# Weights' low halves on VectorE in two pieces, projection products in unbroken halves: a change to the recurrence stage of a transformer block kernel

## The chip, the cores and the metric

One core of one Trainium2 chip. The metric is device time in microseconds (us) of one execution, here the median of several runs. The engines go by the names of the profile: PE (TensorE matmul), PEld (its weight loads), DVE (VectorE), ACT (ScalarE), POOL (GpSimd), SP (SyncE, which issues all DMAs here). "q" behind an engine's name means its queue.

## The reference, cut to what matters

Two transformer blocks on 512 tokens of width 1024, all in float32. The first block is: feed-forward (SwiGLU, inner width 2816), a mixer, feed-forward again. The second is a two-layer hybrid. The change is in the first block's mixer, which projects the normalised input by one wide matrix and feeds the columns to two branches: an RWKV-7 recurrence over time, with 16 heads of 64, and a dilated attention.

```
h = rms_norm(x, mix_norm)
p_rwkv, p_q, p_k, p_v, p_gate = split(h @ w_in)
y_a = rwkv7_time_mix(p_rwkv, ...)
    state = state * w_t + (state @ a_t) b_t + v_t k_t      # 512 steps, per head
    out_t = state @ r_t
y_b = dilated_attention(p_q, p_k, p_v, ...)
merged = g_a * (y_a @ w_proj_rwkv) + g_b * (y_b @ w_proj_attn)
x = x + merged @ w_out
```

## The kernel before, in words

**Products in three parts.** Every large product is made with float32 operands split in a high half (`whi`, `HH`), rounded to the type that PE takes in one pass, and the rest (`wlo`, `HL`). `mm3` (L613) issues three matmuls for one 128x128 block of weights: high by high, high by low, low by high. A block of weights comes as a tile of 128x1024, that is 8 blocks: `wload` (L569) loads it with one DMA on SP into `wraw` (2 buffers), and `wsplit` (L577) makes `whi` by a copy on ACT and `wlo = wraw - whi` by one subtraction of 128x1024 (3 buffers each). The subtraction runs on POOL unless `on` is set; the recurrence stage does not set it. `wnext` (L597) hands out the tile that is due, splits one further tile ahead and loads two ahead (`wfill`, L587).

**The recurrence stage** (`rwkv`, L1175) runs five tasks side by side:

- `rw_stream` (L1233): 24 projection tiles r, k, v, three for each of 8 pairs of heads; `rw_fill` (L1247): 18 tiles of q, k, v for the attention, with a chain of small steps behind each (`qkv_chain`), and 16 tiles of gates. All 58 go through `rw_tile` (L1210): it takes one of two PSUM buffers (`prj`), gets the weights, and issues 8 times `mm3`, 24 matmuls of 512 columns.
- `rw_prep` (L1261): decays, normalised keys and the matrices of 64-step chunks, 8 chunks a pair (`pA` on PE, masked into `AA` on DVE).
- `rw_solve` (L1389), once for each pair: inverts triangular 32x32 blocks. It loads `AS` by 4 DMAs, sets its diagonal (memset on DVE), then 31 times a product `pr` and a sum `Tt` on DVE, each reading the one before; writes `Tt` out by DMA (`scrT`), reads it back transposed (`TB`), makes two groups of 32 small matmuls (`pZ`, a copy on ACT, `pW`, a copy on ACT). `AS` has one buffer, and the copy behind `pZ` lies in it: the next pair's `AS` is loaded only when `pW` is done.
- `rw_chunks` (L1435): the recurrence, 8 chunks for each pair, needs the solve of its pair. A chunk is a chain: `po` on PE, a copy `pp` on ACT, `pu` on PE, a copy into `SV` on ACT, `pS` and a second `po` on PE, and the new state `SV = se + pS` on DVE, with `se` made on POOL.

**What sets the order.** `drive` (L437) plans with estimated durations: each task is a generator that yields the engine it needs next, and the task whose start plus its allowance is least takes the next step. The chunks have allowance 0, the solve 300 ns, the prep 600, `rw_stream` 2000 and `rw_fill` 5000 (`RW_PRIO`, L18). `rw_tile` yields after every `mm3` but the last, so a projection tile is eight steps of 3 matmuls. The framework's scheduler then sets the order of each engine's queue at compile time: of the instructions that its own estimate has ready, the one with the lowest priority number goes first. The number counts up as the program is traced (`cur_priority`); `RW_LATE` (L19) adds 500 to what the two projection tasks issue. Each queue then runs in that fixed order.

Of the kernel before, what the change touches and what calls it, by code (L numbers as in the profile page):

```python
# [7 lines left out]
F32 = mybir.dt.float32  # L8
# [8 lines left out]

RW_PRIO = {"stream": 2000, "fill": 5000}  # L18
RW_LATE = {"rw_stream": 500, "rw_fill": 500, "qkv_chain": -1000}  # L19
FF1_LATE = {"norm": -500, "stats": -300, "mod_steps": 500}  # L20
FF2_PRIO = 300
X_LATE = {"proj_steps": 1000, "taps": 1000, "out_steps": 300}
# [414 lines left out]
def drive(k, tasks):  # L437

    clk, plan, flags = k.clk, k.plan, k.flags
    live = {}
    n = 0

    def hint(x, y):
        x[3] = None
        if isinstance(y, tuple):
            x[3], y = y[:2], y[2]
        x[2] = clk.last
        if y.startswith("+"):  # L450
            y, x[2] = y[1:], 0.0
        x[5] = y.startswith("w")
        x[4] = y.lstrip("w")

    k.born = list(tasks)
    while live or k.born:
        for prio, y, g in k.born:
            live[n] = x = [prio, g, 0.0, None, "PE", False]
            hint(x, y)
            n += 1  # L460
        k.born = []
        if plan.recording:
            best = None
            for i, x in live.items():
                if x[5] and k.held:
                    continue
                r = x[2]
                if x[3] is not None:
                    w = flags.get(*x[3])
                    if w is None:  # L470
                        continue
                    r = max(r, w)
                s = clk.soon(x[4], r) + x[0]
                if best is None or s < best[0]:
                    best = (s, i)
            assert best is not None, ("tasks wait for one another", [(x[1].gi_code.co_name, x[3:]) for x in live.values()])
            i = best[1]
            plan.steps.append(i)
        else:
            i = plan.steps[plan.si]  # L480
            plan.si += 1
        x = live[i]
        assert x[3] is None or flags.get(*x[3]) is not None, "order of tasks"
        clk.last = 0.0
        late = k.late.get(x[1].__name__, 0)
        k.tc._tc.cur_priority += late
        try:
            y = next(x[1])
        except StopIteration:
            del live[i]  # L490
            continue
        finally:
            k.tc._tc.cur_priority -= late
        hint(x, y)
# [32 lines left out]
class K:  # L527
# [49 lines left out]
    def wsplit(self, raw, a, b, on):  # L577
        nc = self.nc
        n = a * b
        hi = self.wp.tile([P, 1024], F32R, tag="whi", name="whi", bufs=3)  # L580
        lo = self.wp.tile([P, 1024], F32R, tag="wlo", name="wlo", bufs=3)
        nc.scalar.copy(hi[:, :n], raw[:, :n])
        (nc.vector if on else nc.gpsimd).tensor_sub(lo[:, :n], raw[:, :n], hi[:, :n].bitcast(F32))
        v = lambda t: t[:, :n].rearrange("p (a b) -> p a b", a=a)
        return v(hi), v(lo)

# [588 lines left out]
    def rwkv(self, H, ya, tw, lad, gd):  # L1175
        nc, tc = self.nc, self.tc
        with ExitStack() as ctx:
# [21 lines left out]
            self.nb["rwmm"], self.nb["qch"] = 2, 1  # L1199
            self.late = RW_LATE  # L1200
            drive(self, [
# [8 lines left out]
    def rw_tile(self, H, w, fin=None, chain=None):  # L1210
        k = self.take("rwmm")
        yield self.need("rwmm", k, "+wPE")
        p = self.rps["mm"].tile([P, T], F32, tag="mm", name="prj")
        w = self.wnext(*w)
        self.held = True
        for x in range(8):
            self.mm3(p, (w[0][:, x], w[1][:, x]), H[x], x == 0, x == 7)
            if x < 7:
                yield "+PE"
        self.held = False  # L1220
        if chain is not None:
            self.spawn(100, "ACT", self.qkv_chain(*chain, p, k))
            return

        def task():
            fin(p)
            self.free("rwmm", k)
            return
            yield

        self.spawn(0, "ACT", task())
# [1191 lines left out]
def body(tc, A, out, plan):  # L2423
    with ExitStack() as ctx:
# [9 lines left out]
        with ExitStack() as lor:  # L2434
            k.lora_setup(lor)
            k.late = FF1_LATE
            with ExitStack() as c2:
# [51 lines left out]
```

## Time and profile before

| | us |
|---|---|
| median of 3 runs | 2654.28 (2636.02 to 2663.36) |
| the profiled execution | 2646.39 |
| its span, first to last instruction | 2644.2 |
| mean granted TensorE clock, share of full speed | 0.927 |

The profiled execution is 2.2 us longer than its span (start and end around the instructions) and lies 7.9 us under the median. The recurrence stage is the stretch from about 442 us, the first projection product, to about 1260 us, the last; the recurrence itself ends at about 1120 us, and what is left of the gate tiles then runs among the attention. All instructions carry the same line (L317, a helper), so groups are told apart by the tiles they write and read: `wlo<-wraw,whi` is the low half of a weight tile.

### The profile page before, as it was taken

What the parts mean: (1) busy time and instruction counts of PE and PEld (TensorE: products, weight loads), DVE (VectorE), ACT (ScalarE), POOL (GpSimd) and SP (SyncE); (2) the same over time, 40 slices, a digit from 0 to 9 for tenths busy, and PEclk for the clock granted to TensorE, in tenths of its full rate; (3) what the DMA queues carried; (4) which work ended last, traced back from release to release, by engine and by line L of the source; (5) the groups of instructions that cost most, each with busy time, mean ns of one, the idle gap of its engine ahead of it and who ended that gap; (6) DMA issues with size and microseconds to landing.
All of it is one profiled execution on the core that took longest, in us unless ns stands there. A gap on an engine that the chain in (4) does not pass through costs nothing. (4 is left out here: it accounts for less than half of the span.)

```text
span 2644.2 us, 33756 instructions
## 1 busy us (share of the span) xinstructions
PE 2442.2 (92%) x12556; PEld 1954.3 (74%) x12556; DVE 1679.8 (64%) x3041; ACT 1017.9 (38%) x1854; POOL 871.1 (33%) x499
## 2 busy tenths in 40 slices
PE   8798999899989998999998999999998999889997
PEld 6576787676667676667777878888777787667776
DVE  8999356556665445443466965674548976569865
ACT  4212234223322223345333444333334555445553
POOL 4444443323221221213442323334423323332331
PEclk9999999879986678889999999999999999899998
DMA  6564333322221112243533333334321112310121
GB/s 208 177 210 162 106 98 107 85 65 76 69 73 49 56 50 80 65 145 97 163 127 104 100 97 111 109 116 132 124 68 43 49 52 72 125 61 25 62 75 51
DMA packets 122196, 254.24 MB, mean 96 GB/s; under 512 B 39208, under 2 KB 54576, under 8 KB 121392
## 3 DMA queue, kind: packets, MB, share of 16 engines
q1 hardware_dynamic: 122032, 252.09, 30.3%
q8 instruction: 99, 1.62, 0.3%
q14 instruction: 65, 0.53, 0.1%
HBM read 222.07 MB, written 21.59 MB: 92 GB/s over the span
## 5 line engine op out<-in xcount | busy, mean ns | idle before, releaser
L317 POOL TENSOR_TENSOR wlo<-wraw,whi 128x1024 fp32r<-128x1024 f32 (+4 forms) x297 | 693.4, 2335 | 1284.5 <-ACT whi L317 1146.9
L317 ACT CAST whi<-wraw 128x1024 fp32r<-128x1024 f32 (+4 forms) x330 | 324.7, 984 | 598.8 <-PE po L317 112.9
L317 PE MATMUL prj<-HH,whi 128*128 128x512 f32 x464 | 214.1, 461 | 0.2 <-DVE v L317 0.2
L317 PE MATMUL prj<-HL,whi 128*128 128x512 f32 x464 | 212.3, 457 | 0.0
L317 PE MATMUL prj<-HH,wlo 128*128 128x512 f32 x464 | 211.5, 456 | 0.0
L317 DVE SCALAR_TENSOR_TENSOR mjunk<-wm,cc 128x1024 f32<-128x1024 f32 x96 | 165.0, 1718 | 6.9 <-DMA wm<-in_l_mod 5.8
L317 PE MATMUL po<-FH,whi 128*128 128x512 f32 x352 | 141.1, 401 | 14.1 <-ACT FH L317 14.1
L317 PE MATMUL pu<-HH,wlo 128*128 128x512 f32 x352 | 138.0, 399 | 10.3 <-POOL wlo L317 10.3
L317 PE MATMUL pg<-HH,whi 128*128 128x512 f32 x352 | 139.7, 397 | 8.2 <-ACT HH L317 7.2
L317 PE MATMUL po<-FL,whi 128*128 128x512 f32 x352 | 140.2, 398 | 0.8 <-DVE FL L317 0.7
L317 PE MATMUL po<-FH,wlo 128*128 128x512 f32 x352 | 139.8, 397 | 1.1 <-POOL wlo L317 1.1
L317 PE MATMUL pg<-HH,wlo 128*128 128x512 f32 x352 | 136.4, 394 | 4.4 <-POOL wlo L317 4.4
L317 PE MATMUL pu<-HH,whi 128*128 128x512 f32 x352 | 140.4, 399 | 0.0
L317 PE MATMUL pg<-HL,whi 128*128 128x512 f32 x352 | 139.3, 396 | 0.7 <-DVE HL L317 0.7
L317 PE MATMUL pu<-HL,whi 128*128 128x512 f32 x352 | 139.7, 397 | 0.0
L317 DVE TENSOR_TENSOR ptl<-pt,pth 128x512 fp32r<-128x512 f32 x156 | 105.0, 684 | 36.5 <-ACT pth L317 35.0
L317 PE MATMUL pj<-HH,whi 128*128 128x512 f32 (+1 forms) x304 | 122.7, 407 | 3.2 <-ACT HH L317 3.2
L317 PE MATMUL pj<-HL,whi 128*128 128x512 f32 (+1 forms) x304 | 122.5, 404 | 0.6 <-DVE HL L317 0.6
L317 PE MATMUL pj<-HH,wlo 128*128 128x512 f32 (+1 forms) x304 | 122.7, 405 | 0.0
L317 ACT ACTIVATE pr<-sc,am 128x768 f32<-128x768 f32 (+1 forms) x120 | 98.0, 818 | 59.1 <-DVE am L317 54.6
L317 DVE TENSOR_TENSOR SV<-se,pS 64x128 f32<-64x128 f32 x56 | 15.6, 279 | 157.8 <-PE pS L317 157.8
L317 PEld LDWEIGHTS prj<-HL,whi 128*128 128x128 f32 x464 | 98.7, 213 | 22.5 <-issue 4.0
(745 smaller groups left out, 6043.6 us busy)
## 6 DMA issues: line engine op xcount, KB each, us to landing
wraw<-in_ffn_w SPq DMA_DIRECT2D x96, 512.0 KB, 3.3
wm<-in_l_mod SPq DMA_DIRECT2D x48, 512.0 KB, 3.4
wraw<-in_l_b SPq DMA_DIRECT2D x45, 512.0 KB, 3.4
wraw<-in_w_rkv SPq DMA_DIRECT2D x24, 512.0 KB, 3.3
wraw<-in_w_qkv SPq DMA_DIRECT2D x18, 512.0 KB, 3.4
wraw<-in_w_gate SPq DMA_DIRECT2D x16, 512.0 KB
wraw<-in_ffn_w SPq DMA_DIRECT2D x16, 448.0 KB, 3.3
xd<-X SPq DMA_DIRECT2D x24, 256.0 KB, 2.0
```

The lines of the kernel that those rows point to most:

```text
L317: r = real(*a, **kw)
```

## The change

Three edits, all in effect only for the 58 tiles of `rw_tile`. First, `rw_tile` asks for its weights with `on=2`: the low half is made on DVE, in two subtractions of 128x512, the first for blocks 0 to 3 and the second for blocks 4 to 7. (Tiles elsewhere with `on=1` stay one subtraction on DVE, those without stay on POOL.) Second, `rw_tile` yields once, after the fourth block, instead of seven times. Third, the matmuls of blocks 1, 2, 3 and 5, 6, 7 get a priority number lower by 3000, those of blocks 0 and 4 keep theirs.

```
+RW_AHEAD = 3000
...
         nc.scalar.copy(hi[:, :n], raw[:, :n])
-        (nc.vector if on else nc.gpsimd).tensor_sub(lo[:, :n], raw[:, :n], hi[:, :n].bitcast(F32))
+
+        for i in range(max(on, 1)):
+            s = slice(i * n // max(on, 1), (i + 1) * n // max(on, 1))
+            (nc.vector if on else nc.gpsimd).tensor_sub(lo[:, s], raw[:, s], hi[:, s].bitcast(F32))
...
-        w = self.wnext(*w)
+        w = self.wnext(*w, on=2)
         self.held = True
         for x in range(8):
+
+            ahead = RW_AHEAD if x % 4 else 0
+            self.tc._tc.cur_priority -= ahead
             self.mm3(p, (w[0][:, x], w[1][:, x]), H[x], x == 0, x == 7)
-            if x < 7:
+            self.tc._tc.cur_priority += ahead
+            if x == 3:
                 yield "+PE"
```

## Rows read from the trace of the kernel before

**Rows 1.** The page: busy time by engine, share of the span, instructions.
```profile
PE 2442.2 (92%) x12556; PEld 1954.3 (74%) x12556; DVE 1679.8 (64%) x3041; ACT 1017.9 (38%) x1854; POOL 871.1 (33%) x499
```

**Rows 2.** Windows: stretch, length, busy PE, PEld, DVE, ACT, POOL, granted clock, DMA.
```profile
510.00:586.00 76.00, 66.77 (x341) 50.94 (x341) 45.58 (x115) 18.17 (x34) 19.33 (x13) 0.76 0.25 66
586.00:657.00 71.00, 66.45 (x396) 49.10 (x397) 42.85 (x134) 24.81 (x50) 22.72 (x18) 0.92 0.25 71
657.00:726.50 69.50, 64.87 (x416) 47.31 (x414) 45.89 (x134) 23.99 (x52) 18.15 (x18) 0.95 0.28 73
726.50:806.00 79.50, 72.19 (x373) 52.73 (x372) 44.82 (x132) 22.03 (x47) 20.17 (x16) 0.76 0.23 64
806.00:892.00 86.00, 83.23 (x390) 60.43 (x389) 44.29 (x119) 21.70 (x48) 18.77 (x16) 0.66 0.21 58
892.00:972.00 80.00, 73.60 (x399) 54.76 (x399) 41.03 (x143) 23.01 (x51) 20.16 (x18) 0.78 0.23 63
972.00:1042.00 70.00, 60.40 (x340) 44.96 (x338) 33.67 (x133) 18.55 (x45) 9.65 (x13) 0.70 0.24 64
1120.00:1260.00 140.00, 134.29 (x611) 100.27 (x610) 56.77 (x112) 69.93 (x169) 36.25 (x16) 0.91 0.39 124
```

**Rows 3.** Timeline of DVE, two starts of a solve: start, duration, [idle before <- releaser].
```profile
585.36 0.28 DVE L317 TENSOR_TENSOR SV<-se,pS 64x128 f32<-64x128 f32 x1 [5.58 <-PE pS L317]
585.62 0.09 DVE L317 MEMSET AS<- 128x32 f32 x1
...
656.11 0.28 DVE L317 TENSOR_TENSOR SV<-se,pS 64x128 f32<-64x128 f32 x1 [0.34 <-PE pS L317]
656.40 0.09 DVE L317 MEMSET AS<- 128x32 f32 x1
```

**Rows 4.** Waits of DVE and of SP's queue, 442 to 1140 us: total, times, longest.
```profile
DVE SV L317 <- PE pS L317: 157.8, 50, 12.3
...
SPq L317 <- POOL wlo L317: 292.3, 39, 25.9
```

**Rows 5.** Windows of PE's `prj` products alone: length, busy (count), granted clock, DMA.
```profile
985.00:1005.00 20.00, 0.00 (x0) 0.50 0.32 73
1005.00:1014.00 9.00, 5.80 (x14) 0.50 0.06 15
1014.00:1024.00 10.00, 5.83 (x20) 0.99 0.34 82
```

**Rows 6.** Timeline of PE at a granted clock of 0.50 and just behind, at 1.00.
```profile
1013.03 0.63 PE L317 MATMUL prj<-HH,wlo 128*128 128x512 f32 x1
1013.46 0.63 PE L317 MATMUL prj<-HH,whi 128*128 128x512 f32 x1
...
1014.49 0.39 PE L317 MATMUL prj<-HH,whi 128*128 128x512 f32 x1
1014.72 0.40 PE L317 MATMUL prj<-HL,whi 128*128 128x512 f32 x1
```

**Rows 7.** Groups of 442 to 1140 us: count | busy, mean ns.
```profile
L317 PE MATMUL prj<-HH,whi 128*128 128x512 f32 x372 | 174.9, 470 | 0.2 <-DVE v L317 0.2
...
L317 POOL TENSOR_TENSOR wlo<-wraw,whi 128x1024 fp32r<-128x1024 f32 x47 | 112.9, 2401 | 233.7 <-ACT whi L317 200.0 <-PE prj L317 14.8 <-issue 8.3
```

**Rows 8.** Timeline of POOL and DVE in solves, where POOL makes a low half.
```profile
514.58 2.08 DVE L317 TENSOR_TENSOR pr<-Tt,AS 128x5 f32<-128x5 f32 x1
...
726.49 2.38 POOL L317 TENSOR_TENSOR wlo<-wraw,whi 128x1024 fp32r<-128x1024 f32 x1
726.66 2.23 DVE L317 TENSOR_TENSOR pr<-Tt,AS 128x3 f32<-128x3 f32 x1
729.11 0.17 DVE L317 TENSOR_TENSOR pr<-Tt,AS 128x4 f32<-128x4 f32 x1
...
1065.91 2.36 DVE L317 TENSOR_SCALAR grr<-gni 128x8 int32<-128x8 int32 x1
```

**Rows 9.** Groups of the whole span by form: the only low halves of 128x512 on DVE.
```profile
L317 DVE TENSOR_TENSOR wlo<-wraw,whi 128x512 fp32r<-128x512 f32 x2 | 1.4, 680 | 0.0
```

## The prediction

> **What bounds the kernel now.** The page comes first: PE is busy for 92% of the span, DVE for 64%, POOL for 33% [rows 1]. That looks like a kernel that only less PE work could shorten. The windows say more [rows 2]. I cut the recurrence at the starts of its solves, so each of the first seven rows is one loop from solve to solve: 76.0, 71.0, 69.5, 79.5, 86.0, 80.0 and 70.0 us, 532 in all. [...] The shortest full loop is the one with the highest clock, the longest the one with the lowest. (The last loop is short at 0.70, but PE issues hardly any products there.)
>
> Why a loop has its length is to be read on DVE. A solve starts with the memset of AS, and before it in DVE's queue stand the state additions of the chunks, each waiting for a product pS [rows 3]. At the low clock one addition waited 5.58 us; at the high one the last before the solve waited 0.34 us. Over the stage these additions hold DVE for 157.8 us in 50 waits [rows 4]. So the loop is: solve on DVE, its result through DMA and through pZ and pW on PE, the reload of AS, and beside that a few chunks whose additions stand ahead of the next solve. PE's clock sets the pace of the chunks and through DVE's queue that of the loop. What is left at 1120 us, PE works off at 96% busy [rows 2]; work that the stage does not finish costs its time there.
>
> **The change part by part.** The working base is the profiled execution, 2646.4 us (span 2644.2 and 2.2 around it), 7.9 under the median of 2654.3.
>
> *Low halves on DVE.* On POOL a tile's low half takes 2401 ns, 47 times in the window [rows 7]. POOL is 33% busy [rows 1], so that looks free. It isn't: a DVE instruction beside it stands still. A pr of 128x3 took 2.23 us while POOL made a low half of 2.38 us, the next, of 128x4, 0.17 [rows 8]. Seventeen of the 47 fall into the eight solves, and in 13 of these cases I find one DVE instruction held, from the pr at 514.58 to the grr at 1065.91, the first and the last of them [rows 8], by 1.9 us on average: 25 us of DVE time on the loop that go away. Added are two pieces of 680 ns [rows 9], 1.36 us a tile, 64 us over the 47. If the same 17 fall into solves they put back 17 x 1.36 = 23 us; if the scheduler finds places for all where DVE is idle (it is busy for 33 to 46 us of a loop [rows 2]), nothing. The bounds are thus -25 and -2, and +23 if the held instructions were covered after all. I take half put back: -25 + 11.5, that is **-13 us**.
>
> [...]
>
> The new wait: PE's third product of a half now waits for DVE's piece, and behind that product stand all later links of the chain. Cover is the tile that is split ahead, 24 products at 0.23 us (the spacing at 1.00 [rows 6]), 5.5 us. If that is used up, a piece that sits behind a state addition waits 157.8/50 = 3.2 us on average [rows 4]. I put it at nothing, and at 3 us a loop for the upper end (+21). SP's queue waits 292 us for POOL's low half, since a load of wraw needs the buffer back [rows 4]; the loads of AS and scrT stand behind it. Two free pieces return it 1.04 us sooner (2.40 - 1.36), held ones later by the 3.2; nothing for the sum, with the same two ends. ACT's copy to whi is unchanged.
>
> *Unbroken halves.* No product goes or comes. Today 3 products stand between two links of a chunk; from now on, once the first three of a half are out, nine more go ahead of any chain instruction. What this can win is clock. From 985 to 1005 us PE had no product at all and ran at 0.50; 14 products in a row from 1005 to 1014 came at 0.50, and behind them it was 0.99 [rows 5]. The spacing fell from 0.43 to 0.23 us on the way [rows 6]. A half is 12 in a row, where the loops at 0.66 to 0.78 had them in threes. If every loop ran like the 657-to-726.5 one, the seven would give 532 - 7 x 69.5 = 45 us. Ends: 0 and -45. I take two thirds, **-30 us**, since pZ, pW and stretches without a product will still drop the clock.
>
> *Links behind a half.* Of a loop, pZ and pW must be passed by PE at once; each can now find up to nine more products ahead: 9 x 0.23 = 2.1 us at the high clock, half on average. For 16 such links, with products under way at six in ten (prj is 55 to 60% of PE's time here by its busy windows: 5.8 of 9 and of 10 us [rows 5]), that is 16 x 1.04 x 0.6 = **+10 us**; ends 0 and 16 x 2.1 = +34. Links of prep are not counted: a pair's pA lies a loop ahead of its solve.
>
> *Fewer yields.* The planner now sees halves as single steps and places them differently; this moves what the queues hold, not how much. Nothing, with no sign that I can defend.
>
> Sum: 2646.4 - 13 - 30 + 10 = 2613.4; I say **2614 us**, 40 under the median.
>
> **The rivals.**
> *Halves in the way (slower).* The additions ahead of a solve wait for chunk links, and a half in front of a link costs 2.1 us at the high clock (3.9 at 0.43 us a product). If each of the four or so chunks ahead of a solve meets one half, a loop grows by 8.4 us, seven by 59. With no clock won and -13 for the low halves: 2646 + 59 - 13 = **2692**. It decides from three halves a loop: 3 x 2.1 x 7 = 44 eats the 43 us of both gains. For it speaks how tightly DVE is tied to pS [rows 4]; against it that the scheduler knows the halves and can put the solve's start ahead of later additions.
> *The clock swings (no change).* Products in clumps leave stretches without any, and such a stretch ran at 0.50 [rows 5]. Then the halves themselves run half their time slow and the chain between them too; won and lost clock cancel: 2646 - 13 + 10 = **2643**. The same comes out if the change doesn't do what it says, because products are not ready when their number is up and the halves break. [...]
> *More than forecast.* All loops at 69.5 (-45), all 25 us of DVE back, links free: 2646 - 70 = **2576**.
>
> **How the numbers follow.** A measurement of this kernel tells about 1% from no change, that is 26.5 us: faster means under 2628, slower over 2681. Forecast 0.50, its own spread 2590 to 2640, so 0.40 faster and 0.10 the same. More 0.10, all faster. Swing 0.22: 0.03 faster, 0.16 same, 0.03 slower. Halves in the way 0.18: 0.04 same, 0.14 slower. Together 0.53, 0.30, 0.17. The range reaches down to 2565, below the third rival, and up to 2685, most of the way to the first, with the upper ends of the waits in it.
>
> **What would show it.** Right: solve-to-solve loops of 70 to 76 us with no clock under 0.8; DVE's small instructions without 2 us outliers beside POOL; state additions waiting for pS well below 157.8 us in total; runs of 12 prj products. Wrong: PE idle before prj with DVE wlo as releaser (the cover gone); pZ, pW or pu late behind products with loops over 80 us at a high clock (first rival); a clock that flips more often with the same mean (second). I am wrong altogether if the loops do not set the stage, and the end comes from the gates' tail after 1120 us.

## The result, and the profile after

The changed kernel takes 2551.4 us (2548.3 to 2555.6), the kernel before beside it 2658.8 (2636.0 to 2666.6): a ratio of 0.961, 95% interval 0.955 to 0.967, and 107 us less from median to median. I had forecast 2614 and a range down to 2565. The direction was right, the size not, and the runs below show that the larger part came from a term that I had priced at 13 us. Ratios are made from the runs within 1.5% of the fastest of their kernel, which leaves out two runs in all: one of four of split with one yield (2569 us), one of ten of the kernel that adds POOL's subtraction to it (2645 us).

The page of the profile after, busy time by engine [rows 1]:

```profile
PE 2372.9 (93%) x12556; PEld 1920.0 (75%) x12556; DVE 1703.2 (67%) x3157; ACT 1014.7 (40%) x1852; POOL 745.1 (29%) x441
```

DVE has 116 instructions more, two for each of 58 tiles, and POOL 58 fewer. PE issues the same 12556 matmuls (one record for each product of two rounded halves, 1392 for the 58 tiles of 24; two for each plain float32 product `pA`, 256 for 128) and is busy 69 us less: it is the same work at a higher clock, 0.948 of full speed over the span for 0.927.

Windows after, cut at the starts of the solves as in [rows 2], and behind them the whole stage from the first projection product to the first product of the attention's output projection, and its two parts:

```profile
489.00:568.00 79.00, 75.10 (x440) 60.74 (x439) 55.23 (x173) 26.99 (x45) 7.41 (x7) 0.96 0.36 104
568.00:640.00 72.00, 70.35 (x452) 54.40 (x450) 48.52 (x154) 27.91 (x57) 8.28 (x11) 0.98 0.33 92
640.00:717.00 77.00, 73.93 (x416) 57.46 (x414) 45.27 (x149) 22.87 (x50) 8.87 (x12) 0.82 0.27 76
717.00:791.00 74.00, 72.99 (x452) 56.62 (x452) 53.91 (x169) 27.74 (x56) 14.86 (x13) 0.95 0.30 80
791.00:874.50 83.50, 81.97 (x462) 62.37 (x461) 50.50 (x158) 28.17 (x55) 7.92 (x12) 0.88 0.27 76
874.50:948.00 73.50, 66.12 (x396) 51.55 (x395) 41.89 (x137) 22.16 (x56) 10.86 (x15) 0.72 0.23 61
948.00:1007.00 59.00, 57.75 (x362) 44.69 (x361) 41.00 (x115) 19.60 (x37) 6.59 (x8) 1.00 0.43 116
...
439.50:1212.40 772.90, 733.20 (x4198) 565.91 (x4196) 465.46 (x1361) 281.07 (x606) 107.62 (x110) 0.90 0.32 92
439.50:1105.00 665.50, 641.80 (x3747) 497.06 (x3745) 416.78 (x1236) 230.64 (x457) 86.33 (x97) 0.91 0.31 90
```

The same stage before:

```profile
442.70:1307.70 865.00, 804.43 (x4188) 603.17 (x4187) 440.67 (x1247) 284.56 (x607) 227.58 (x166) 0.83 0.28 82
```

The seven loops sum to 518 us, 14 less than before. That is all that the bound of my prediction, the loop from solve to solve, gave. The stage is 92 us shorter. Where the rest lies is seen in the projection products alone, up to the recurrence's end and after it. Before:

```profile
442.70:1120.00 677.30, 357.11 (x1060) 0.81 0.24 67
1120.00:1307.70 187.70, 95.71 (x334) 0.93 0.43 136
```

After:

```profile
439.50:1105.00 665.50, 371.72 (x1392) 0.91 0.31 90
1105.00:1212.40 107.40, 0.00 (x0) 0.81 0.33 110
```

Before, about 334 of the 1392 products were left for the time after the recurrence; now none is, and what follows is 80 us shorter. They found room inside a recurrence that is 12 us shorter than it was, because PE stood still less and ran faster. An account that closes, as an estimate: PE's idle time in the stage is its length less its busy time, 60.6 us before and 39.7 after. Read in windows of 1 us, the clock is 0.50 or 1.00 in 821 of the stage's 865 windows before and in 747 of 773 after, in the others between the two. Taken as these two values alone, the time at the low clock is twice the length times the clock's lack, 2 x 865.0 x 0.17 = 294 and 2 x 772.9 x 0.10 = 155 (summed over the windows, 287 and 157). With products 0.43 us apart at 0.50 and 0.23 at 1.00 [rows 6], about half of it is lost. So 20.9 + 139/2 = 90 of the 92 us, or 86 by the sums over the windows. (Time at the low clock in which PE idles is counted twice by this; it is 6 to 8 us of loss in both.) Outside the stage nothing moved: 440 us ahead of it, 1337 and 1341 behind.

In the other waits, state additions now hold DVE for a third of the 157.8 us of [rows 4] (which edit did that is seen below), SP waits for DVE where it waited for POOL, and the copy behind `pu`, one link of the chunk chain, waits longer than before (57.2 us in 55 waits):

```profile
DVE SV L318 <- PE pS L318: 51.6, 37, 5.3
...
SPq L318 <- DVE wlo L318: 243.3, 43, 22.8
...
ACT SV L318 <- PE pu L318: 88.7, 56, 4.9
```

### The profile page after: what moved, and what is told of

Same layout as the page of the kernel before. It is cut to its first block, busy times and chain, and to the rows that moved or that the text cites. A ratio compares the mean times of both kernels' runs of the same rounds, so it can differ in the third digit from the quotient of the medians.

```text
span 2553.8 us, 33817 instructions
## 1 busy us (share of the span) xinstructions
PE 2372.9 (93%) x12556; PEld 1920.0 (75%) x12556; DVE 1703.2 (67%) x3157; ACT 1014.7 (40%) x1852; POOL 745.1 (29%) x441
## 4 chain that ended last, share of the span: by engine, by line
PE 68%; DVE 19%; ACT 4%; issue 4%; DMA 2%; POOL 2%; SPq 0%; DVEq 0%; ACTq 0%; POOLq 0%
PE prj L318 12%; PE po L318 11%; PE pj L318 7%; PE pu L318 6%; PE pg L318 6%; DVE mjunk L318 5%; PE pm L318 4%; PE pwo L318 4%; PE sc L318 3%; PE pt L318 2%; DVE c0cy L318 1%; DVE fb L318 1%; PE pA L318 1%; DMA wm<-in_l_mod 1%; PE pl L318 1%
## 5 line engine op out<-in xcount | busy, mean ns | idle before, releaser
L318 POOL TENSOR_TENSOR wlo<-wraw,whi 128x1024 fp32r<-128x1024 f32 (+5 forms) x239 | 552.3, 2312 | 1012.6 <-ACT whi L318 926.4
L318 PE MATMUL prj<-HH,whi 128*128 128x512 f32 x464 | 197.4, 426 | 0.0
L318 PE MATMUL prj<-HH,wlo 128*128 128x512 f32 x464 | 190.9, 412 | 0.0
L318 PE MATMUL prj<-HL,whi 128*128 128x512 f32 x464 | 187.4, 404 | 0.0
L318 DVE TENSOR_TENSOR wlo<-wraw,whi 128x512 fp32r<-128x512 f32 (+1 forms) x149 | 122.5, 832 | 41.6 <-ACT whi L318 35.8
L318 POOL TENSOR_TENSOR se<-SV,EC 64x128 f32<-64x128 f32 x56 | 36.3, 648 | 302.4 <-DVE SV L318 238.8
```

What stands on the lines that cost most here:

```text
L318: r = real(*a, **kw)
```

## The experiments

The change has three edits: the split (low halves on DVE, two pieces), the yield (one step border a tile instead of seven) and the priority step. Every ratio is to the kernel before on the same chip, with its 95% interval.

**One edit at a time.** The split alone, that is the changed kernel with

```
-            ahead = RW_AHEAD if x % 4 else 0
+            ahead = 0
...
-            if x == 3:
+            if x < 7:
                 yield "+PE"
```

> Low halves on DVE in two pieces, products as before (threes, seven yields). If the gain comes from DVE being freed of POOL's hold (DVE theory), most of the 107 us is here: 2560 to 2590, with the state additions' wait near the changed kernel's 51.6 us. If it comes from the unbroken halves (run theory), this is a few us from before: 2635 to 2660, granted clock of the stage near 0.83, and about 300 of the 1392 products still left when the recurrence ends.

The halves alone, low halves back on POOL (`w = self.wnext(*w)`):

> Halves unbroken, low halves back on POOL in one piece. Run theory: nearly all of the gain, 2555 to 2590, stage clock 0.88 to 0.91, all products out before the recurrence ends. DVE theory: little, 2630 to 2660. If the two need each other, both this and the split alone gain less than half.

Split and yield, without the priority step (`ahead = 0`):

> As changed, but no priority step: the planner sees two steps a tile, the scheduler may still break the halves. If the planner's order alone moves the products forward (planner theory), this is 2555 to 2590 with runs of products still in ones and twos on PE. If the unbroken run matters, 2620 to 2660.

Split and priority step, with seven yields (`if x < 7`):

> As changed, but with seven yields: the priority step alone makes the runs. Run theory: 2550 to 2580, runs of 12. Planner theory: 2620 to 2660.

The yield alone, on POOL and without the priority step, came in the next group:

> One yield a tile, no priority step, low halves on POOL. Split with one yield gave 2527, the split alone 2580, so one yield is worth 52 beside the split. If the two add, this is 2646 - 52 = 2595; if the planner's order pays only where DVE is free of POOL, 2625 to 2650.

| | low halves on POOL | on DVE, two pieces |
|---|---|---|
| seven yields | 1 (the kernel before) | 0.9745 (0.9693 to 0.9796) |
| seven yields, priority step | not run | 0.9796 (0.9744 to 0.9847) |
| one yield | 0.9814 (0.9773 to 0.9854) | 0.9511 (0.9428 to 0.9593) |
| one yield, priority step | 0.9869 (0.9808 to 0.9930) | 0.9611 (0.9548 to 0.9673) |

Read down and across, the table is nearly additive. The split gives 2.6, 3.0 and 2.6 points in its three pairs; the yield 1.9, 2.3 and 1.9. The priority step, which alone makes the halves unbroken, seems to cost: 0.5, 1.0 and 0.5 points. Each of these three lies within the intervals, but all have one sign, and side by side on one chip the runs with seven yields do not overlap (2577 to 2586 us without the step, 2591 to 2597 with it). So neither the run theory nor the DVE theory in its plain form held; split and yield each do about what they do without the other.

A sign of the DVE theory missed too. In the split alone the state additions' wait did not come near the changed kernel's 51.6 us, and the shortest such wait stands in the halves on POOL, a slower kernel:

```profile
DVE SV L318 <- PE pS L318: 135.2, 52, 8.6
```

```profile
DVE SV L318 <- PE pS L318: 46.1, 22, 5.6
```

Up to the end of the recurrence it is 46 to 70 us in the three kernels of the table with the priority step, and 85 to 158 in the four without it. It is shortest where the priority step is, and the time does not go with it.

The priority step does what it says. In the timeline of PE I counted the stretches of projection products with nothing between: 311 before, 146 after, 46 of them of exactly 12; in the run with priority and seven yields also 146, in split with one yield 245 and mostly of one to four. Longer runs did not buy clock. Stage windows of the split alone, and with the priority step added:

```profile
439.40:1240.30 800.90, 764.74 (x4196) 575.95 (x4195) 450.67 (x1361) 284.68 (x608) 99.49 (x110) 0.87 0.31 89
```

```profile
439.20:1249.50 810.30, 760.79 (x4197) 585.10 (x4196) 469.43 (x1361) 279.90 (x606) 98.08 (x110) 0.86 0.30 88
```

Idle time 36 and 50 us, clock 0.87 and 0.86. What a run may cost is seen in the chain: the copy behind `pu` waits 88.7 us in the changed kernel and half of that in split with one yield, whose stage is the shorter one:

```profile
ACT SV L318 <- PE pu L318: 42.7, 48, 2.4
```

```profile
439.50:1194.40 754.90, 734.49 (x4196) 555.91 (x4195) 452.65 (x1361) 280.99 (x606) 99.82 (x110) 0.91 0.33 95
```

With one yield and the low halves on POOL this wait is 71 us with the priority step against 44 without, with seven yields on DVE only 60 against 57, so it is not the whole of it.

**Is it POOL's hold?** I had seen DVE's instructions held beside POOL's low half, 25 us in the solves, and had let the new pieces on DVE eat half of that up. The split alone gave 67 us. To tell the hold from everything else that the split alters, POOL makes its subtraction once more, where nobody reads it:

```
         nc.scalar.copy(hi[:, :n], raw[:, :n])
...
+        if on == 2:
+            nc.gpsimd.real.tensor_sub(raw[:, :n], raw[:, :n], hi[:, :n].bitcast(F32))
```

(`real` passes the planner by, so its steps stay.)

> The split alone, and POOL besides makes its old subtraction of 128x1024 once more for each of the 58 tiles, in place in wraw, behind DVE's pieces; nobody reads the result (it is left out of the computation). DVE theory (POOL's hold on DVE is what the split took away): the time goes most of the way back, from 2580 to 2620 or more, with DVE instructions of 2 us beside POOL again. Order theory (the split gains because planner and scheduler order the queues otherwise): it stays within 15 us of 2580, since the planner is not told of POOL's work. The buffer of wraw also comes back some 2.4 us later, as before the change.

It gave 0.9958 (0.9938 to 0.9978): of the split's 2.6 points 0.4 are left. But this run also gives `wraw` back later and gives the scheduler one more instruction. The control puts two memsets of the same buffer in its place, 2 x 957 ns, which wait for the same instructions and read nothing:

```
+        if on == 2:
+            for _ in range(2):
+                nc.gpsimd.real.memset(raw[:, :n], 0.0)
```

> The split alone, and behind DVE's pieces POOL sets wraw to zero, twice, in the place where the run with the subtraction put it (nobody reads it). It waits for the same instructions and gives wraw back later too (by the two memsets, an estimated 2 us), but reads nothing from SBUF. Hold theory: 2570 to 2600, as the split alone (2580), with no DVE instruction lengthened beside the memsets. Buffer or order theory: 2620 to 2650, as with the subtraction (2642).

0.9666 (0.9609 to 0.9722): no loss. Both once more on split with one yield, from another order of the queues:

> Split and one yield (2527), with POOL's subtraction added as before. Hold theory: the loss is 50 to 75 us here too, 2577 to 2602, near one yield on POOL (2607). If the earlier loss came from one unlucky order, under 2560.

> Split and one yield (2527), with the two memsets of wraw on POOL. Hold theory: 2515 to 2545. Buffer or order theory: near the run with the subtraction, 2575 or more.

With the subtraction 0.9909 (0.9871 to 0.9947), with the memsets 0.9561 (0.9511 to 0.9610), without either 0.9511. The subtraction cost 4 points here, more than I expected, the memsets half a point within the intervals. Buffer and extra instruction are out. What is left is that the subtraction reads two tiles where the memset reads none (and takes 2.43 us a tile for 1.91), and so, by exclusion, the hold. That others wait longer for a POOL that is busier is not it: in the stage PE, DVE and ACT together wait 5.5 us for POOL in the split alone and 7.3 with the subtraction. The solve's products `pr` show it by themselves, 248 small instructions whose work is the same in all kernels. Before:

```profile
L317 DVE TENSOR_TENSOR pr<-Tt,AS 128x2 f32<-128x2 f32 (+30 forms) x248 | 106.9, 431 | 5.1
```

The split alone:

```profile
L318 DVE TENSOR_TENSOR pr<-Tt,AS 128x2 f32<-128x2 f32 (+30 forms) x248 | 89.0, 359 | 4.5
```

With POOL's subtraction added to it, then one case of the hold from its timeline:

```profile
L589 POOL TENSOR_TENSOR wraw<-wraw,whi 128x1024 f32<-128x1024 f32 x54 | 131.2, 2429 | 272.7 <-DVE wlo L318 142.1 <-issue 25.6 <-ACT sq L318 14.4
L318 DVE TENSOR_TENSOR pr<-Tt,AS 128x2 f32<-128x2 f32 (+30 forms) x248 | 112.8, 455 | 4.5
```

```profile
618.09 0.35 DVE L318 TENSOR_TENSOR pr<-Tt,AS 128x100 f32<-128x100 f32 x1
618.32 2.36 POOL L589 TENSOR_TENSOR wraw<-wraw,whi 128x1024 f32<-128x1024 f32 x1 [12.09 <-DVE wlo L318]
...
618.77 2.10 DVE L318 TENSOR_TENSOR pr<-Tt,AS 128x105 f32<-128x105 f32 x1
```

With the memsets:

```profile
L590 POOL MEMSET wraw<- 128x1024 f32 x114 | 109.1, 957 | 281.7 <-issue 76.8 <-DVE wlo L318 60.4 <-DVE Mg L318 34.8
...
L318 DVE TENSOR_TENSOR pr<-Tt,AS 128x2 f32<-128x2 f32 (+30 forms) x248 | 88.9, 358 | 4.3
```

106.9, 89.0, 112.8 and 88.9 us: the hold goes with the split, comes with POOL's subtraction, and does not come with POOL's memset. Its own size is only these 18 to 24 us and, against what each group usually takes, some 35 us on other DVE instructions (DVE is busy for 511.5 us of the stage, for 450.7 in the split alone). The memsets lengthened DVE instructions too, which I had not expected: by DVE's busy time in the stage, 466.1 us, some 15 us in all, none of it on `pr`, and with no loss of time. So held time as such is not the price; it matters which instructions are held. The stage of the run with the subtraction shows what it turns into:

```profile
441.80:1312.20 870.40, 803.80 (x4196) 604.01 (x4195) 511.45 (x1364) 285.19 (x610) 236.22 (x167) 0.83 0.28 82
```

Against the split alone PE idles 67 us instead of 36 and runs at 0.83 instead of 0.87, that is, by the same estimate, 2 x 870.4 x 0.17 = 296 us at the low clock instead of 208: 31 + 44 = 75 us, of 70 by which the stage is longer. That held DVE instructions make PE wait is seen in PE's waits. The longest that DVE ends, in the split alone and with the subtraction added:

```profile
PE pA L318 <- DVE BK L318: 4.9, 1, 4.9
PE pz L318 <- DVE dqx L318: 1.6, 1, 1.6
PE py L318 <- DVE Og L318: 1.0, 2, 0.9
```

```profile
PE pA L318 <- DVE BK L318: 9.3, 2, 7.4
PE py L318 <- DVE Og L318: 6.6, 4, 2.9
PE pz L318 <- DVE dqx L318: 5.8, 1, 5.8
```

All such waits in the stage sum to 28 us before, 8 in the split alone, 32 with the subtraction and 15 with the memsets; with one yield to 37 on POOL, 12 on DVE, 35 with the subtraction and 14 with the memsets. So 24 of the 31 us of idle time are waits for DVE. That these waits also cost PE its clock is the reading that fits; I have not traced single cases from a hold to a drop of the clock.

**Planner or queue?** The split also changes what the planner is charged. With the split on DVE and POOL's price in the plan:

> The split alone, with the planner still charged POOL's price, so the steps are planned as before; only the scheduler knows of DVE. If the planner's new steps make the split's gain: 2630 to 2660. If not: 2570 to 2595.

0.9819 (0.9764 to 0.9874), between the two expectations. Most of the split's gain needs no new plan; whether the new plan adds 0.7 points is not settled, the intervals overlap.

**What does one yield do?** My theory was that a longer step gets the products planned earlier. A step of the whole tile (no yield at all), and seven yields with the allowances of the projection tasks cut to a quarter (`RW_PRIO = {"stream": 500, "fill": 1250}`), both with the split and without the priority step:

> Split, no priority step, and no yield within a tile: the planner sees one step of 24 products. If a longer step takes the products further ahead (planner theory), 2500 to 2540, with more than 409 of the 1392 products out by 600 us. If a long step costs the chain more than it wins, over 2550. Seven yields gave 2580, one gave 2527.

> Split, seven yields in threes, no priority step, and the planner's allowances for the two projection tasks cut to a quarter (500 and 1250 for 2000 and 5000). If one yield works by planning the products earlier, this gets most of the same by other means: 2530 to 2560, and the products are out before the recurrence ends. If the length of the step itself is what counts, it stays at 2570 to 2600.

No yield gave 0.9523 (0.9483 to 0.9563), the same as one, but with 384 products out by 600 us where I wanted over 409. The cut allowances gave 0.9936 (0.9906 to 0.9965), against my theory. Its products are early indeed, all out by 1072 us, but the recurrence then ran on to 1201 alone:

```profile
441.60:1072.50 630.90, 407.12 (x1392) 0.87 0.30 88
1072.50:1201.30 128.80, 0.00 (x0) 0.60 0.13 34
```

The early products pushed the recurrence back and left it these 128.8 us without any, at a clock of 0.60. One yield brought both forward: split with one yield ends its recurrence at 1082 us with all products out, the split alone at 1097 with 1176. (All products out is not needed for it: with no yield the recurrence ends as early with 1321 out, in the same time.) Why it strikes that balance is left open; that products be early is not enough.

**Pieces, and the rest of POOL.** One piece of 128x1024 on DVE, one yield, no priority step (`on=1`):

> Split and one yield, but the low half in one piece of 128x1024 on DVE (1222 ns against 2 x 680). If the pieces matter (a state addition waits behind a shorter one), 2540 to 2570; if not, within 15 us of 2527, or under it by up to 5 for the shorter total on DVE.

0.9517 (0.9483 to 0.9551): the pieces make no difference that these runs can show. On top of that, the products `AR` and `BB` and the sum `y` moved from POOL to DVE:

> Split in one piece, one yield, no priority step, and three further operations of the prep and the tail moved from POOL to DVE (the products AR and BB and the sum y, 8 of each). Their holds are some 14 of the 22 us by which DVE's instructions are still lengthened; on DVE they cost about 8 x (1.2 + 0.7 + 0.7) = 21 us, most of it beside waits. Hold theory at its plainest: 2505 to 2525; if DVE's own load counts as much, 2524 to 2540.

0.9671 (0.9604 to 0.9738), worse by 1.5 points, and worse than either expectation. The solve's `pr` took 86.1 us for 86.9 without this move, so they show hardly any hold that went with it; what the three cost on DVE, or in the order that came of them, was more. I did not take that apart.

Three of these are the fastest, and cannot be told apart: split with one yield in two pieces (0.9511), in one (0.9517), and with no yield (0.9523), each without the priority step. Against the changed kernel (0.9611) each is about a point better, with intervals that just overlap.

## Why the prediction was wrong

*What bounds the kernel.* The step that failed first. I took the loop from solve to solve as the stage's bound and said that the end would come from the gates' tail only if I was wrong altogether. That is what happened: the seven loops gave 14 us, the tail 80. In split with one yield the eight solves themselves even take longer than before (350 us from first `pr` to last `Tt`, summed, against 317), and the kernel is 4.9% faster. With the yield alone the seven loops are longer than before (553 us against 532), and the kernel is 1.9% faster. The wait through which I had PE's clock pace the loop, of the state additions for `pS` (5.58 us at a clock of 0.50 and 0.34 at 1.00 in the two cases that I cited), is shortest in the kernels with the priority step, which won no time. By the estimate above, what the stage costs is the same PE work throughout, plus PE's idle time, plus half the time at the low clock: taking these two off the stage's length leaves 657 us before, 656 after, 661 for the split, 667 with one yield, 656 with the hold put back. Over all sixteen kernels it leaves 631 to 673; with the low clock counted only while PE is busy, it leaves 657 to 672.

*Low halves on DVE*, -13 us. The cause was right (POOL's subtraction put back by itself took `pr` from 89.0 to 112.8 us), and so was the hold's size in the solves: 25 us, of which `pr` alone shows 18 to 24. This is the term that was most mis-sized: measured alone it is 67 us. What failed is the price. I set a microsecond of held DVE at a microsecond of the loop, as the loop was my bound, and charged DVE's pieces in the same coin. Even with all 25 us free and nothing charged, the term would have been under half. The hold put back alone cost 56 and 106 us: held instructions kept PE waiting (32 us of waits for DVE instead of 8, 35 instead of 12 with one yield), and its clock was lower besides (0.83 for 0.87, 0.84 for 0.91). That the pieces cost so little because scheduler and planner know of them, while the hold is in no estimate, is argued and not shown.

*The new wait* of PE for DVE's piece, priced at nothing: right. PE never idles before a product with `wlo` in the changed kernel, and in the split with seven yields and with one no idle time of PE ends with DVE's low half. SP's queue waits 243 us for low halves instead of 292, also nothing to see in the time.

*Unbroken halves*, -30 us of clock: not won. Runs of 12 came with no higher clock than short ones (0.86 against 0.87, above), and all three pairs are slower with them. I had kept a third back for `pZ`, `pW` and stretches without a product: in windows of 1 us the clock fell to 0.50 within 6 us of the start of `pZ` in four of the eight solves before and in two after; that `pZ` or `pW` brought it down was not shown. Nor did the kernel before have its products in threes, as I wrote: 204 of its 311 stretches hold one or two. With low halves on POOL the halves did bring 1.3 points, some 35 us, but that this is near my -30 is luck: the yield alone brought 1.9. The clock of the changed kernel rose from 0.83 to 0.90, and the split and the yield each raised it (0.83 to 0.87 either way), the priority step did not.

*Links behind a half*, +10 us: the right sign and, if the priority step's 0.5 to 1.0 points (13 to 26 us) are the price of the links, not far under. In two of three pairs it shows at the link after `pu`; that it stands at `pZ` and `pW`, as I had it, was not seen. (The share of six in ten was read too high: the two windows cited give 64% and 58%, but the seven loops 33 to 58%.)

*Fewer yields*, nothing: wrong. They are worth 1.9 to 2.3 points, some 50 us. With them PE idled 58 us for 61 on POOL and 20 for 36 on DVE, and its clock rose by 0.04 in both; how the planner's order does this stays open. The stage of the yield alone:

```profile
442.90:1262.00 819.10, 761.08 (x4186) 571.86 (x4186) 430.31 (x1248) 283.31 (x607) 230.78 (x166) 0.87 0.30 87
```

*The rivals.* Halves in the way was, if the priority step's cost is that, small beside the other two edits. The swing of the clock did not come: the low time fell from 294 to 155 us. "More than forecast" came closest, with the wrong reason: I gave it 45 us for the loops and 25 for DVE, where the loops gave 14.

## What to carry to other kernels

When PE has filler work that may run at any time, read the stage by PE's account (idle time, and the time that it lost at the low clock, by the estimate above half of what it was busy there) and ask what is left over at its end, not only for the loop that looks serial. POOL, 33% busy, was no free place here for a subtraction of 128x1024 while the solve's chain of small instructions ran on DVE (a `pr` took 431 ns on average, and 359 in the split alone); but three further operations moved off POOL cost 1.5 points. Put a suspected cost back by itself, with a control that shares all but the suspected property: here that turned a hold that I had put at 25 us into a measured 56 and 106 (2.1 and 4.0 points of some 2650). An edit of the same change may cost: in all three pairs the kernel is 0.5 to 1.0 points better without the priority step, each time within the intervals.

## What the hardware showed that I had not expected

What DVE lost beside POOL depended here on what POOL did. The subtraction of 2.43 us lengthened the solve's products `pr`, two memsets of 0.96 us did not (112.8 and 88.9 us for the group, 89.0 with neither). Some other DVE instructions were lengthened beside the memsets, though, such as these two, which took 0.17 us each in all twelve cases of the changed kernel and here end with the memsets:

```profile
599.89 1.97 POOL L590 MEMSET wraw<- 128x1024 f32 x2 [4.74 <-issue]
600.03 0.84 DVE L318 TENSOR_SCALAR dqi<-dqx 128x8 int32<-128x8 int32 x1
...
600.91 0.98 DVE L318 TENSOR_SCALAR drk<-dqi 128x8 int32<-128x8 int32 x1
```

Over the run the 12 `drk<-dqi` took 507 ns on average. Why these were lengthened and `pr` was not, the runs do not show.
